# Another order of the expert slots in a unit, routing two units ahead, and the left sums of a block on its own partitions

## The chip, the cores and the metric

The kernel runs on one core of one Trainium2 chip. The metric is the device time of one execution in microseconds (us); the time before is the median of three runs.

## The reference

Two transformer blocks follow each other, for 256 tokens of width 2048 in float32. The change touches the expert layer of the second block (`peer_ffn`) and the place behind it, where the gate of the last layer is multiplied. Each token has 8 heads; for each head the reference picks 16 of 16,384 experts, takes the dot product of each expert's row `u` with the token, and adds up the rows `v` weighted by a gate.

```python
def peer_ffn(x, w_peer_q, peer_subkeys, peer_u, peer_v):
    q = (x @ w_peer_q).reshape(B, S, PEER_HEADS, 2, PEER_HALF)
    s = jnp.einsum('bshcd,hcnd->bshcn', q, peer_subkeys)
    top_s, top_i = lax.top_k(s, PEER_TOPK)
    cand = top_s[..., 0, :, None] + top_s[..., 1, None, :]
    ...
    best_s, best_c = lax.top_k(cand, PEER_TOPK)
    i1 = jnp.take_along_axis(top_i[..., 0, :], best_c // PEER_TOPK, axis=-1)
    i2 = jnp.take_along_axis(top_i[..., 1, :], best_c % PEER_TOPK, axis=-1)
    experts = i1 * N_KEYS + i2
    gates = jax.nn.softmax(best_s, axis=-1)
    ...
        u = peer_u[ec]
        act = jax.nn.gelu(jnp.einsum('tkd,td->tk', u, xc))
        return jnp.einsum('tk,tkd->td', gc * act, peer_v[ec])

    h = h + peer_ffn(rms_norm_2(h, ffn_norm[l]), ...)
    gate = jax.nn.sigmoid(rms_norm_2(h, ple_norm[l]) @ w_ple_gate[l])
    h = h + gate * (p[l] @ w_ple_proj[l])
```

The 16 experts of a head come out of `top_k` in the order of their gates: rank 0 has the largest, rank 15 the smallest. The inputs make the softmax steep, so that many gates of high rank are zero in float32.

## The kernel before

Most of the kernel is a row of matrix products whose weights stream from HBM (`gemm`, L343): each weight tile is loaded by SP, split into a rounded part by ACT (`h_...`, L361) and a rest by DVE (`l_...`, L362), and three matmuls of PE (L371 to L373) use them. `w_pg` is the last of these products and comes right behind the expert layer.

The expert layer is `peer` (L1310). It works in 4 blocks `u` of 64 tokens and in 4 pairs of heads `g`, which gives 16 units, `(0, 0)`, `(0, 1)` and so on; this document numbers them 0 to 15. In a unit, partitions 0 to 63 hold the 64 tokens for the first head of the pair and partitions 64 to 127 the same tokens for the second. A unit has 16 slots. Slot `j` handles one expert for each of the 128 partitions: rank `j` on the lower half and rank `(j + 8) % 16` on the upper half, since `route` writes the upper half's lists with the two groups of eight exchanged (L1478 to L1480). The slots are taken in the order 0, 8, 1, 9, 2, 10 up to 7, 15.

`slot` (L1386) does the work of one slot:

- POOL gathers 128 rows of 16 KB (`u` and `v` of an expert side by side) into one of `UVB` = 6 buffers `uvb` (L1390). A row whose gate is below the smallest normal float gets an index out of bounds, and the gather skips it. The first three slots of either group of eight in unit 0 skip nothing, so that all six buffers hold finite numbers.
- DVE multiplies the 2048 columns of `u` by the token `xg` and sums them (L1394). This document calls it the product of a slot.
- ACT takes the gelu, multiplies by the gate, and writes the result on a diagonal `dgs` (L1395 to L1398).
- PE multiplies `dgs` with the 2048 columns of `v` and adds to `acc_e` in PSUM (L1403). The left 1024 columns go to partitions 0 to 63 of `acc_e`, the right ones to 64 to 127.

POOL's queue holds nothing but the gathers in this stage, and they are issued in the order of the slots; a gather waits until PE is done with the slot six before it, whose buffer it fills.

`route` (L1418) finds the experts of a unit: four matmuls, then about 35 small DVE instructions for the two `top_k` and the look-up of indices, and a softmax. It is a generator, and `peer` runs a step of it after slots 0, 1, 3, 4, 6 and 7 for the unit to come. The order of the program text does not set the order of instructions, though: a scheduler places them, engine by engine, by its own estimate of when each is ready.

`block_x` (L1357) writes the tokens of a block, scaled, into `xg` and copies them to the other half of the partitions by a move on SP's queue. `block_out` (L1370) ends a block. A block `u` belongs to token half `t = u // 2` and stands on partitions `a * 64` to `a * 64 + 63` of `h`, with `a = u % 2`. ACT copies the half of `acc_e` that lies on the other partitions to `mv` (L1376), SP moves it over (L1377), and DVE adds both halves to `h`, 1024 columns each (L1379, L1380). For an odd block the half that has to be moved is the left one. `half_out` (L1382) squares and sums 512 columns of a token half (ACT, L340), transposes them on PE (L1412) and splits them by ACT and DVE (L309, L310) into the operands of `w_pg`; token half 0 is done inside the last unit's loop, half 1 behind it.

Of the kernel before, what the change touches and what calls it, by code (L numbers as in the profile page):

```python
# [13 lines left out]
ALU = mybir.AluOpType  # L14
# [251 lines left out]
class Net:  # L266
# [1043 lines left out]
    def peer(self):  # L1310

        nc, F, tc = self.nc, self.F, self.tc
        with tc.tile_pool(name="stg", bufs=2) as self.stg, tc.tile_pool(name="gat", bufs=1) as gat:
            self.gat = gat
            self.lists = {}
            for _ in self.route(0, 0):  # L1320
                pass
            xg = {0: self.block_x(0)}
            uv = [gat.tile([P, 2 * D], F32, tag=f"uv{i}", name=f"uvb{i}") for i in range(UVB)]
            junk = F(mybir.dt.bfloat16, (P, D))
            ssqp = self.small([P, 2, 4], keep="ssqe")
            order = [r + 8 * i for r in range(8) for i in range(2)]
            units = [(u, g) for u in range(4) for g in range(4)]
            acc = {}
            slot = 0
            for i, (u, g) in enumerate(units):  # L1330
                if g == 0:
                    acc[u] = self.psa.tile([P, 1024], F32, tag="acc", name=f"acc_e{u}")
                if g == 3 and u < 3:
                    xg[u + 1] = self.block_x(u + 1)
                later = self.route(*units[i + 1]) if i < 15 else iter(())
                for k, j in enumerate(order):
                    self.slot(u, g, j, uv[slot % UVB], xg[u], junk, acc[u], k == 0, k == 15)
                    slot += 1
                    if k in (0, 1, 3, 4, 6, 7):
                        next(later, None)  # L1340
                    if g == 0 and k == 2 and u:
                        self.block_out(u - 1, acc[u - 1])
                    if i == 15 and k in (3, 6, 9, 12):
                        if k == 3:
                            F.free(*self.qT, *self.sk, *self.gf)
                            n = Ops(F, 16, self.fp)
                        self.half_out(n, ssqp, 0, k // 3 - 1)
                for _ in later:
                    pass
            self.block_out(3, acc[3])  # L1350
            for c in range(4):
                self.half_out(n, ssqp, 1, c)
            F.free(junk)
        self.dump("x5", self.h)
        self.n4, self.rs4 = n, self.res_rs(ssqp)

    def block_x(self, u):  # L1357

        nc = self.nc
        t, a = u // 2, u % 2  # L1360
        x = self.gat.tile([P, D], F32, tag="xg", bufs=2, name=f"xg{u}")
        s, o = slice(a * 64, a * 64 + 64), slice(64 - a * 64, 128 - a * 64)
        for i in range(2):
            c = slice(i * 1024, (i + 1) * 1024)
            nc.vector.scalar_tensor_tensor(x[s, c], self.h[s, t, c], self.rs3[s, t:t + 1], self.gf[i][s], op0=ALU.mult,
                                           op1=ALU.mult)
        nc.sync.dma_start(x[o], x[s])
        return x

    def block_out(self, u, acc):  # L1370

        nc = self.nc
        t, a = u // 2, u % 2
        s, o = slice(a * 64, a * 64 + 64), slice(64 - a * 64, 128 - a * 64)
        e = self.gat.tile([P, 1024], F32, tag="mv", name=f"mv{u}")
        nc.scalar.copy(e[o], acc[o])  # L1376
        nc.sync.dma_start(e[s], e[o])  # L1377
        own, far = self.h[s, t, a * 1024:(a + 1) * 1024], self.h[s, t, (1 - a) * 1024:(2 - a) * 1024]
        nc.vector.tensor_tensor(own, acc[s], own, op=ALU.add)  # L1379
        nc.vector.tensor_tensor(far, e[s], far, op=ALU.add)  # L1380

    def half_out(self, n, ssqp, t, c):  # L1382
        self.sq_acc(self.h[:, t, c * 512:(c + 1) * 512], ssqp[:, t, c:c + 1])
# [2 lines left out]
    def slot(self, u, g, j, b, xg, junk, acc, begin, end):  # L1386
        nc, stg = self.nc, self.stg
        nm = f"{u}_{g}_{j}"
        idx, gate = self.lists[u, g]
        nc.gpsimd.indirect_dma_start(out=b, out_offset=None, in_=self.ap["uv"],  # L1390
                                     in_offset=bass.IndirectOffsetOnAxis(ap=idx[:, j:j + 1], axis=0),
                                     bounds_check=N_EXPERTS - 1, oob_is_err=False)
        a = stg.tile([P, 4], F32, tag="act", bufs=8, name=f"act{nm}")
        nc.vector.scalar_tensor_tensor(junk, b[:, :D], 1.0, xg, op0=ALU.mult, op1=ALU.mult, accum_out=a[:, 0:1])  # L1394
        nc.scalar.activation(a[:, 2:3], a[:, 0:1], AF.Gelu_apprx_tanh)  # L1395
        nc.scalar.activation(a[:, 3:4], a[:, 2:3], AF.Copy, scale=gate[:, j:j + 1])
        dg = stg.tile([P, 64], F32, tag="dgs", bufs=6, name=f"dgs{nm}")
        nc.scalar.activation(dg, self.c("id2"), AF.Copy, scale=a[:, 3:4])  # L1398
        first, last = g == 0 and begin, g == 3 and end
        for c in range(2):  # L1400
            for i in range(2):
                o = D + i * 1024 + c * 512
                nc.tensor.matmul(acc[i * 64:(i + 1) * 64, c * 512:(c + 1) * 512], dg, b[:, o:o + 512],  # L1403
                                 start=first, stop=last)

    def half_ops(self, ops, t, g, gname):
# [154 lines left out]
```

## Time and profile before

| | |
|---|---|
| three runs | 3237.61, 3239.88, 3243.05 us; median 3239.88 |
| the profiled execution, its own time | 3243.22 us |
| span of the profile (first to last instruction) | 3241.5 us |
| busy PE, DVE, ACT, POOL | 2879.1, 2164.7, 1438.7, 544.7 us |
| granted TensorE clock, mean | 0.966 |
| expert stage, first to last product L1394 | 2260.5 to 3123.3 us of the span |
| units 0, 1 to 8, 9 to 15 | 81.8, 428.9, 352.1 us |

The profile is of one execution. A share of busy time is a mean over the stage or window that it is given for. A row of a timeline has its start in us from the start of the span, its length, engine, line, operation, and in brackets the idle time of that engine before it and what ended it. `PEclk` is the granted clock of TensorE as a share of the full one.

### The profile page before, as it was taken

The page shows a single profiled execution, that of the slowest core. Times are in us where ns is not written, and L with a number is a line of the kernel's source. Part 1 is how long each engine was busy: PE and PEld are TensorE (multiplying, and loading weights), DVE is VectorE, ACT ScalarE, POOL GpSimd, SP SyncE. Part 2 cuts the span into 40 slices and gives each one's busy share as a digit, 9 for nine tenths or more (in the row PEclk, how much of TensorE's full clock was granted, in tenths as well). Part 3 has the DMA queues.
Part 4 walks back from the last instruction along what each step waited for, and adds up shares of the span by engine and source line. Part 5 has one row for each costly group of instructions (what it writes and reads, how often), then busy time and mean ns, then how long its engine had stood idle before and what let it go on. Part 6 is the DMA issues. An engine that isn't in the chain of part 4 may idle for free. (4 is left out here: it accounts for less than half of the span.)

```text
span 3241.5 us, 45843 instructions
## 1 busy us (share of the span) xinstructions
PE 2879.1 (89%) x17372; PEld 2268.3 (70%) x17372; DVE 2164.7 (67%) x3089; ACT 1438.7 (44%) x2464; POOL 544.7 (17%) x320
## 2 busy tenths in 40 slices
PE   8999999999999999999999999996566666666668
PEld 8888888989898998999999998896111111111136
DVE  7769666554545455686444577656989788877765
ACT  5446665434444444575434444542333233322244
POOL 0000000000000000011000021000355445564611
PEclk9999999999999999999999999998798988999999
DMA  7645564666666666656666545764688888878874
GB/s 261 182 150 188 157 183 143 184 193 183 193 185 192 183 189 185 185 173 185 184 182 182 158 148 164 213 184 150 259 313 309 304 331 284 332 294 332 319 257 142
DMA packets 156397, 691.86 MB, mean 213 GB/s; under 512 B 34127, under 2 KB 36431, under 8 KB 139855
## 3 DMA queue, kind: packets, MB, share of 16 engines
q1 hardware_dynamic: 119312, 425.64, 43.2%
q0 software_dynamic: 36864, 263.29, 21.7%
q8 instruction: 137, 2.24, 0.3%
q14 instruction: 84, 0.69, 0.1%
HBM read 955.12 MB, written 4.19 MB: 296 GB/s over the span
## 5 line engine op out<-in xcount | busy, mean ns | idle before, releaser
L1403 PE MATMUL acc_e<-uvb,dgs 128*64 128x512 f32 x2048 | 554.0, 672 | 303.5 <-ACT dgs L1398 303.5
L1394 DVE SCALAR_TENSOR_TENSOR f<-uvb,xg 128x2048 bf16<-128x2048 f32 x256 | 586.5, 2291 | 136.6 <-DMA uvb<-in_uv,idx 122.4
L1403 PEld LDWEIGHTS acc_e<-uvb,dgs 128*64 128x64 f32 x2048 | 138.2, 149 | 710.1 <-ACT dgs L1398 523.7
L1390 POOL DMA_INDIRECT uvb<-in_uv,idx x256 | 431.6, 1686 | 669.3 <-PE acc_e L1403 319.5
L1395 ACT ACTIVATE act<-act 128x1 f32<-128x1 f32 x256 | 51.9, 203 | 544.2 <-DVE f L1394 544.1
L381 PE MATMUL acc_w_up<-f,l_w_up 128*128 128x256 f32 x1024 | 289.9, 283 | 0.0
L378 PE MATMUL acc_w_up<-f,h_w_up 128*128 128x256 f32 x1024 | 289.9, 283 | 0.0
L380 PE MATMUL acc_w_up<-f,h_w_up 128*128 128x256 f32 x1024 | 289.8, 283 | 0.0
L362 DVE TENSOR_TENSOR l_w_up<-r_w_up,h_w_up 128x1024 fp32r<-128x1024 f32 x128 | 165.8, 1295 | 175.7 <-PE acc_w_up L381 153.1
L362 DVE TENSOR_TENSOR l_w_down<-r_w_down,h_w_down 128x1024 fp32r<-128x1024 f32 x128 | 161.2, 1260 | 162.2 <-PE acc_w_down L372 133.4
L361 ACT CAST h_w_down<-r_w_down 128x1024 fp32r<-128x1024 f32 x128 | 135.1, 1055 | 197.8 <-PE acc_w_down L373 168.5
L361 ACT CAST h_w_up<-r_w_up 128x1024 fp32r<-128x1024 f32 x128 | 134.7, 1052 | 196.6 <-PE acc_w_up L380 175.6
L371 PE MATMUL acc_w_down<-h_w_down,f 128*128 128x512 f32 x512 | 199.6, 390 | 0.0
L372 PE MATMUL acc_w_down<-l_w_down,f 128*128 128x512 f32 x512 | 199.5, 390 | 0.0
L373 PE MATMUL acc_w_down<-h_w_down,f 128*128 128x512 f32 x512 | 199.2, 389 | 0.0
L380 PEld LDWEIGHTS acc_w_up<-f,h_w_up 128*128 128x128 f32 x1024 | 196.6, 192 | 0.1
L378 PEld LDWEIGHTS acc_w_up<-f,h_w_up 128*128 128x128 f32 x1024 | 196.6, 192 | 0.1
L381 PEld LDWEIGHTS acc_w_up<-f,l_w_up 128*128 128x128 f32 x1024 | 196.6, 192 | 0.0
L584 POOL TENSOR_TENSOR f<-f 128x1024 f32<-128x1024 f32 x16 | 30.3, 1894 | 802.9 <-ACT f L583 802.9
L373 PEld LDWEIGHTS acc_w_down<-h_w_down,f 128*128 128x128 f32 x512 | 96.1, 188 | 19.9
L372 PEld LDWEIGHTS acc_w_down<-l_w_down,f 128*128 128x128 f32 x512 | 96.1, 188 | 19.8
L371 PEld LDWEIGHTS acc_w_down<-h_w_down,f 128*128 128x128 f32 x512 | 96.1, 188 | 19.7
(555 smaller groups left out, 7812.2 us busy)
## 6 DMA issues: line engine op xcount, KB each, us to landing
r_w_up<-in_w_up SPq DMA_DIRECT2D x128, 512.0 KB, 3.7
r_w_down<-in_w_down SPq DMA_DIRECT2D x128, 512.0 KB, 4.1
r_w_qkv<-in_w_qkv SPq DMA_DIRECT2D x48, 512.0 KB, 3.7
r_w_xbc<-in_w_xbc SPq DMA_DIRECT2D x32, 512.0 KB, 4.1
r_w_xr<-in_w_xr SPq DMA_DIRECT2D x32, 512.0 KB, 3.7
r_w_yr<-in_w_yr SPq DMA_DIRECT2D x32, 512.0 KB, 3.6
r_w_gr<-in_w_gr SPq DMA_DIRECT2D x32, 512.0 KB, 3.6
r_w_ro<-in_w_ro SPq DMA_DIRECT2D x32, 512.0 KB, 3.6
```

Of the source, the lines that this page charges most:

```text
L361: nc.scalar.copy(wh, raw)
L362: nc.vector.tensor_sub(wl, raw, wh.bitcast(F32))
L371: nc.tensor.matmul(o, xh[:, s], h, start=first, stop=False)
L372: nc.tensor.matmul(o, xh[:, s], l, start=False, stop=False)
L373: nc.tensor.matmul(o, xl[:, s], h, start=False, stop=fin)
L378: nc.tensor.matmul(o, wh[:, s], xh, start=first and b % 2 == 0, stop=False, skip_group_check=True)
L380: nc.tensor.matmul(o, wh[:, s], xl, start=False, stop=False, skip_group_check=True)
L381: nc.tensor.matmul(o, wl[:, s], xh, start=False, stop=fin, skip_group_check=True)
L1390: nc.gpsimd.indirect_dma_start(out=b, out_offset=None, in_=self.ap["uv"], in_offset=bass.IndirectOffsetOnAxis(ap=idx[:, j:j + 1], axis=0), ...
L1394: nc.vector.scalar_tensor_tensor(junk, b[:, :D], 1.0, xg, op0=ALU.mult, op1=ALU.mult, accum_out=a[:, 0:1])
L1395: nc.scalar.activation(a[:, 2:3], a[:, 0:1], AF.Gelu_apprx_tanh)
L1403: nc.tensor.matmul(acc[i * 64:(i + 1) * 64, c * 512:(c + 1) * 512], dg, b[:, o:o + 512], start=first, stop=last)
```

## The change

The slots of units 1 to 15 are taken in the order 0, 15, 8, 7, 1, 14, 9, 6, 2, 13, 10, 5, 3, 12, 11, 4; unit 0 keeps its order. Routing is written two units ahead: unit 0 runs the steps for units 1 and 2, one after each slot, and unit `i` those for unit `i + 2`, after slots 1, 3, 5, 8, 10 and 13. `half_out` of token half 0 moves from the last unit to the one before. In an odd block the two halves of `acc_e` change places, so that the left sums always lie on the block's own partitions and the right ones are moved; and the sums to `h` are made in four pieces of 512 columns, left ones first.

```diff
@@ -1323,7 +1324,7 @@
             uv = [gat.tile([P, 2 * D], F32, tag=f"uv{i}", name=f"uvb{i}") for i in range(UVB)]
             junk = F(mybir.dt.bfloat16, (P, D))
             ssqp = self.small([P, 2, 4], keep="ssqe")
-            order = [r + 8 * i for r in range(8) for i in range(2)]
+            even = [0, 15, 8, 7, 1, 14, 9, 6, 2, 13, 10, 5, 3, 12, 11, 4]
             units = [(u, g) for u in range(4) for g in range(4)]
             acc = {}
             slot = 0
@@ -1332,15 +1333,15 @@
                     acc[u] = self.psa.tile([P, 1024], F32, tag="acc", name=f"acc_e{u}")
                 if g == 3 and u < 3:
                     xg[u + 1] = self.block_x(u + 1)
-                later = self.route(*units[i + 1]) if i < 15 else iter(())
-                for k, j in enumerate(order):
+                later = self.routes(units[i + 2:i + 3] if i else units[1:3])
+                for k, j in enumerate(even if i else [r + 8 * h for r in range(8) for h in range(2)]):
                     self.slot(u, g, j, uv[slot % UVB], xg[u], junk, acc[u], k == 0, k == 15)
                     slot += 1
-                    if k in (0, 1, 3, 4, 6, 7):
+                    if i == 0 or k in (1, 3, 5, 8, 10, 13):
                         next(later, None)
                     if g == 0 and k == 2 and u:
                         self.block_out(u - 1, acc[u - 1])
-                    if i == 15 and k in (3, 6, 9, 12):
+                    if i == 14 and k in (3, 6, 9, 12):
                         if k == 3:
                             F.free(*self.qT, *self.sk, *self.gf)
                             n = Ops(F, 16, self.fp)
@@ -1354,6 +1355,11 @@
         self.dump("x5", self.h)
         self.n4, self.rs4 = n, self.res_rs(ssqp)
 
+    def routes(self, units):
+        for u in units:
+            yield from self.route(*u)
+            yield
+
     def block_x(self, u):
 
         nc = self.nc
@@ -1375,9 +1381,9 @@
         e = self.gat.tile([P, 1024], F32, tag="mv", name=f"mv{u}")
         nc.scalar.copy(e[o], acc[o])
         nc.sync.dma_start(e[s], e[o])
-        own, far = self.h[s, t, a * 1024:(a + 1) * 1024], self.h[s, t, (1 - a) * 1024:(2 - a) * 1024]
-        nc.vector.tensor_tensor(own, acc[s], own, op=ALU.add)
-        nc.vector.tensor_tensor(far, e[s], far, op=ALU.add)
+        for c in range(4):
+            hc = self.h[s, t, c * 512:(c + 1) * 512]
+            nc.vector.tensor_tensor(hc, (acc if c < 2 else e)[s, (c % 2) * 512:(c % 2 + 1) * 512], hc, op=ALU.add)
 
     def half_out(self, n, ssqp, t, c):
         self.sq_acc(self.h[:, t, c * 512:(c + 1) * 512], ssqp[:, t, c:c + 1])
@@ -1400,7 +1406,8 @@
         for c in range(2):
             for i in range(2):
                 o = D + i * 1024 + c * 512
-                nc.tensor.matmul(acc[i * 64:(i + 1) * 64, c * 512:(c + 1) * 512], dg, b[:, o:o + 512],
+                p = 64 * (i ^ (u % 2))
+                nc.tensor.matmul(acc[p:p + 64, c * 512:(c + 1) * 512], dg, b[:, o:o + 512],
                                  start=first, stop=last)
 
     def half_ops(self, ops, t, g, gname):
```

The lines behind L1316 are shifted by one to seven in the new kernel; the product is L1400 there.

On DVE, the rows at the start of unit 3 (the names `act_3_8` and so on give head pair and slot of a product; `tv`, `tiu`, `cand`, `best`, `bc` are routing), before:

```order
L1496 MAX tv_24230<-mr_24251 128x8
L1497 MAX_INDEX tiu_24231<-tv_24230,mr_24251 128x8
L1441 CAST tif_24283<-tiu_24231 128x32
L1443 TENSOR_TENSOR cand_24285<-tv_24230 128x256
L1493 MAX best_24287<-cand_24285 128x8
L1394 SCALAR_TENSOR_TENSOR f_301_21721,act_3_8_22581<-uvb_21716,xg_21711 128x2048
L1493 MAX tv_24782<-sc_24780 128x8 x2
L1494 MAX_INDEX bc_24288<-best_24287,cand_24285 128x8
L1494 MAX_INDEX tiu_24783<-tv_24782,sc_24780 128x8 x2
L1394 SCALAR_TENSOR_TENSOR f_301_21721,act_3_1_22600<-uvb_21717,xg_21711 128x2048
L1394 SCALAR_TENSOR_TENSOR f_301_21721,act_3_9_22613<-uvb_21718,xg_21711 128x2048
L1394 SCALAR_TENSOR_TENSOR f_301_21721,act_3_2_22638<-uvb_21719,xg_21711 128x2048
```

and now:

```order
L1503 MAX tv_24032<-mr_24073 128x8
L1504 MAX_INDEX tiu_24033<-tv_24032,mr_24073 128x8
L1448 CAST tif_24105<-tiu_24033 128x32
L1450 TENSOR_TENSOR cand_24107<-tv_24032 128x256
L1500 MAX best_24109<-cand_24107 128x8
L1400 SCALAR_TENSOR_TENSOR f_301_21721,act_3_15_22632<-uvb_21716,xg_21711 128x2048
L1500 MAX tv_24587<-sc_24585 128x8 x2
L1501 MAX_INDEX bc_24110<-best_24109,cand_24107 128x8
L1501 MAX_INDEX tiu_24588<-tv_24587,sc_24585 128x8 x2
L1400 SCALAR_TENSOR_TENSOR f_301_21721,act_3_8_22660<-uvb_21717,xg_21711 128x2048
L1400 SCALAR_TENSOR_TENSOR f_301_21721,act_3_7_22673<-uvb_21718,xg_21711 128x2048
L1400 SCALAR_TENSOR_TENSOR f_301_21721,act_3_1_22692<-uvb_21719,xg_21711 128x2048
```

The products have another slot in each place; the routing instructions between them are of the same kind and stand in the same places.

On ACT, behind the last slot of the expert stage (`mv` is the copy of `block_out`, `junk` the squares, `f_...<-ho_ple_norm` an operand half of `w_pg`, `h_w_pg_0` the rounded first weight tile), before:

```order
L1376 COPY mv_26140<-acc_e_25036 64x1024
L340 ACTIVATE junk_26145,ssqe_21722<-h 128x512
L340 ACTIVATE junk_26160,ssqe_21722<-h 128x512
L309 ACTIVATE f_302_25923<-ho_ple_norm_1_0_26147,pv 128x128
L340 ACTIVATE junk_26175,ssqe_21722<-h 128x512
L309 ACTIVATE f_304_25979<-ho_ple_norm_1_1_26162,pv 128x128
L309 ACTIVATE f_302_25923<-ho_ple_norm_1_0_26147,pv 128x128
L340 ACTIVATE junk_26190,ssqe_21722<-h 128x512
L361 CAST h_w_pg_0_26249<-r_w_pg_0_26248 128x1024
```

and now, from the eighth row behind that copy on:

```order
L309 ACTIVATE f_302_25721<-ho_ple_norm_1_0_26155,pv 128x128
L309 ACTIVATE f_306_25833<-ho_ple_norm_1_2_26185,pv 128x128
L309 ACTIVATE f_304_25777<-ho_ple_norm_1_1_26170,pv 128x128
L317 ACT_TABLE_LOAD
L317 ACTIVATE s_26218<-s_26217 128x2
L309 ACTIVATE f_308_25889<-ho_ple_norm_1_3_26200,pv 128x128
L309 ACTIVATE f_302_25721<-ho_ple_norm_1_0_26155,pv 128x128
L309 ACTIVATE f_306_25833<-ho_ple_norm_1_2_26185,pv 128x128
L309 ACTIVATE f_304_25777<-ho_ple_norm_1_1_26170,pv 128x128
L309 ACTIVATE f_308_25889<-ho_ple_norm_1_3_26200,pv 128x128
L361 CAST h_w_pg_0_26257<-r_w_pg_0_26256 128x1024
L309 ACTIVATE f_306_25833<-ho_ple_norm_1_2_26185,pv 128x128
```

The cast of the first weight tile stood eighth behind the copy; now it stands eighteenth, behind eight more operand halves, a table load and a root.

## Rows read from the trace of the kernel before

**Rows 1.** The page, DMA queues: packets, MB, share of 16 engines.

```profile
q0 software_dynamic: 36864, 263.29, 21.7%
```

**Rows 2.** Windows of units 1 to 8: header, and the sum of the eight.

```profile
core 0: us, PE busy (x) PEld busy (x) DVE busy (x) ACT busy (x) POOL busy (x), PEclk, DMA share, GB/s
...
sum 428.90, PE 280.79 PEld 71.27 DVE 373.81 ACT 145.18 POOL 218.14; mean PE 35.10 PEld 8.91 DVE 46.73 ACT 18.15 POOL 27.27
```

**Rows 3.** Windows of units 9 to 15: the sum of the seven.

```profile
sum 352.10, PE 231.33 PEld 58.77 DVE 263.38 ACT 98.82 POOL 180.55; mean PE 33.05 PEld 8.40 DVE 37.63 ACT 14.12 POOL 25.79
```

**Rows 4.** Windows, units 9 to 15: sums of four quarters; unit 11's third.

```profile
sum 91.90, PE 57.93 PEld 15.21 DVE 66.22 ACT 25.59 POOL 45.55; mean PE 8.28 PEld 2.17 DVE 9.46 ACT 3.66 POOL 6.51
...
sum 95.10, PE 57.61 PEld 14.17 DVE 65.44 ACT 22.14 POOL 44.33; mean PE 8.23 PEld 2.02 DVE 9.35 ACT 3.16 POOL 6.33
...
2898.30:2910.60 12.30, 8.27 (x30) 2.04 (x26) 9.21 (x9) 3.29 (x12) 6.88 (x4) 0.86 0.57 196
...
sum 82.10, PE 54.31 PEld 13.49 DVE 64.46 ACT 22.59 POOL 39.47; mean PE 7.76 PEld 1.93 DVE 9.21 ACT 3.23 POOL 5.64
...
sum 83.10, PE 61.48 PEld 15.91 DVE 67.26 ACT 28.59 POOL 51.19; mean PE 8.78 PEld 2.27 DVE 9.61 ACT 4.08 POOL 7.31
```

**Rows 5.** The same for units 1-3 and 5-7; unit 7's third quarter.

```profile
sum 82.30, PE 47.33 PEld 12.96 DVE 80.71 ACT 17.16 POOL 16.37; mean PE 7.89 PEld 2.16 DVE 13.45 ACT 2.86 POOL 2.73
...
sum 68.30, PE 52.73 PEld 12.85 DVE 55.16 ACT 24.46 POOL 57.08; mean PE 8.79 PEld 2.14 DVE 9.19 ACT 4.08 POOL 9.51
...
2689.60:2699.60 10.00, 8.62 (x32) 2.39 (x32) 9.20 (x8) 3.40 (x13) 5.42 (x4) 0.83 0.69 247
sum 69.00, PE 47.09 PEld 11.73 DVE 55.31 ACT 18.34 POOL 40.48; mean PE 7.85 PEld 1.95 DVE 9.22 ACT 3.06 POOL 6.75
...
sum 85.60, PE 58.01 PEld 14.35 DVE 79.24 ACT 40.11 POOL 53.47; mean PE 9.67 PEld 2.39 DVE 13.21 ACT 6.68 POOL 8.91
```

**Rows 6.** Timeline of DVE at the start of unit 1: its first three products.

```profile
2342.26 2.28 DVE L1394 SCALAR_TENSOR_TENSOR f<-uvb,xg 128x2048 bf16<-128x2048 f32 x1
...
2347.96 2.27 DVE L1394 SCALAR_TENSOR_TENSOR f<-uvb,xg 128x2048 bf16<-128x2048 f32 x1
...
2351.47 2.27 DVE L1394 SCALAR_TENSOR_TENSOR f<-uvb,xg 128x2048 bf16<-128x2048 f32 x1
```

**Rows 7.** Timeline around 2970: two products, the first one's matmuls, the next issue.

```profile
2967.86 2.29 DVE L1394 SCALAR_TENSOR_TENSOR f<-uvb,xg 128x2048 bf16<-128x2048 f32 x1
...
2970.25 2.29 DVE L1394 SCALAR_TENSOR_TENSOR f<-uvb,xg 128x2048 bf16<-128x2048 f32 x1
...
2971.16 1.94 PE L1403 MATMUL acc_e<-uvb,dgs 128*64 128x512 f32 x8 [0.45 <-ACT dgs L1398]
...
2973.71 2.09 POOL L1390 DMA_INDIRECT uvb<-in_uv,idx  x1 [0.30 <-issue]
```

**Rows 8.** First gather (POOL, timeline), its product, and DMA view of 2254 to 2276.

```profile
2252.10 1.16 POOL L1390 DMA_INDIRECT uvb<-in_uv,idx  x1 [242.69 <-DVE tv L1493]
...
2260.54 2.29 DVE L1394 SCALAR_TENSOR_TENSOR f<-uvb,xg 128x2048 bf16<-128x2048 f32 x1 [0.87 <-DMA uvb<-in_uv,idx]
...
DMA packets 624, 9.17 MB, mean 417 GB/s; under 512 B 64, under 2 KB 64, under 8 KB 64
```

**Rows 9.** Chain of waits (first three) and ACT's timeline behind the last slot.

```profile
3126.25 1.01 ACT mv L1376
3127.28 2.83 DMA mv<-mv
3130.14 1.23 DVE h L1380
...
3134.97 1.04 ACT L361 CAST h_w_pg<-r_w_pg 128x1024 fp32r<-128x1024 f32 x1
...
3135.92 1.13 ACT L309 ACTIVATE f<-ho_ple_norm,pv 128x128 fp32r<-128x128 f32 x4
...
3137.07 1.28 ACT L317 ACT_TABLE_LOAD   x1
```

## The prediction, made before the run

> **What bounds the kernel now.** The page comes first: the software queue, which carries the gathers, moved 263.29 MB [rows 1]. Every edit lies in the expert stage or just behind it, so I cut that stage into its sixteen units, each from the first product L1394 of one unit to that of the next, and read the windows view of them. The reader is to see that DVE has two kinds of unit. Units 1 to 8 last 428.9 us with DVE busy 373.81, units 9 to 15 last 352.1 with DVE busy 263.38 [rows 2, 3]: 55.1 and 88.7 us of waiting. A unit of the first kind holds some 45 us of DVE work, one of the second some 37; the difference is routing.
>
> Next I cut each unit into four quarters of four slots. In units 9 to 15 DVE idles 25.7, 29.7, 17.6 and 15.8 us in the four quarters, summed over seven units (window minus DVE busy) [rows 4]. So it waits most where the gathers are largest, but the lightest quarter still idles 2.5 us a unit, and there the DMA share is down to 0.57 in unit 11 [rows 4]. Not all of the waiting is load, then. In units 1 to 3 and 5 to 7 the same sums are 1.6, 13.1, 13.7 and 6.4 [rows 5]: the first quarter hardly waits, since routing fills DVE there while gathers land.
>
> The timeline shows it: at the start of unit 1 the products begin 5.7 and 3.5 us apart instead of the bare 2.4, because routing stands between, and none of them waited for a DMA [rows 6]. What landed during this burst feeds the products behind it.
>
> Last, the ring of six buffers. A product is followed by three ACT instructions and eight matmuls: one began at 2967.86, the next 2.39 later, its matmuls ended at 2973.10, 5.2 after its start, and then POOL issued for 2.09 [rows 7]. At one product per 2.39 us the ring allows 6 x 2.39 = 14.3 us a turn; 5.2 + 0.3 + 2.1 are spent, which leaves 6.7 for landing. A full gather of 2.10 MB needed 7.3 (issue ended at 2253.26, product began at 2260.54), and the transfers run at 417 GB/s while six such gathers are queued [rows 8].
>
> **Sizes of the slots.** Rows with a vanished gate are skipped. Evaluating the reference's routing on its inputs gives the share of rows kept by rank: 1.00, 0.95, 0.88, 0.78 for ranks 0 to 3, 0.37 for rank 8, 0.13 for rank 15. Slot j has rank j below and (j+8) mod 16 above, so slots 0 and 8 fetch about 87 rows, 1 and 9 82, 2 and 10 74, and 7 and 15 only 37. In the old order the first six slots of a unit ask for 486 rows and the last six for 254; in the new order any six ask for about 370. The total is unchanged (16,066 rows of 16 KB are the 263.29 MB).
>
> **Routing two units ahead: 0 us.** The order of the built programs settles this. The routing burst stands at the same places on DVE in both, behind the last product of a unit and its first two; the scheduler had already run it far ahead. What the new code interleaves over slots 1 to 13 does not appear there. Nothing is added to or taken from POOL or SP: 256 gathers, four moves of xg and four of mv, at the same slots. Half of the operands of tokens 0 to 127 now come a few slots earlier in unit 8, with the same instructions, hidden in its 53.53 us of DVE work; if that cover went it would only change places.
>
> **The order of the slots, units 9 to 15: -7 us.** No burst hides anything here. If every quarter idled like the two lighter ones, (25.7 + 29.7) - (17.6 + 15.8) = 22 us would go; that is the lower bound, and 0 the upper. An evened quarter carries more than the light ones do, and these idle 2.4 us a unit anyway, so I take a third: -7.
>
> **The order of the slots, units 1 to 8: +11 us.** The burst lets six slots land. They used to be the heaviest; now 116 rows fewer (1.9 MB) are fetched under it, and have to be fetched later beside products. At 417 GB/s that is 4.6 us a unit at most. At the low end the second and third quarters would idle like a light quarter of units 9 to 15, 2.4 each, against (13.1 + 13.7) / 6 = 4.5 together now: +0.3. With the mean quarter of units 9 to 15 (88.7 / 28 = 3.2) it is +1.9. Since the DMA has slack in these quarters (a share of 0.69 in unit 7's third) [rows 5], I take 1.4, between the two: 8 x 1.4 = 11, bounds +2 and +36. Unit 0 keeps its order.
>
> **The left sums stay: +1 us.** Four sums of 512 columns in place of two of 1024 cost nothing new: one of 1024 takes 1.23 [rows 9], so one of 512 about 0.6 (an estimate from that row). At the end of block 3 the left sums no longer wait for the move: copy 1.01 and move 2.83 [rows 9], -3.8 if all of it were saved. But PE transposes all four chunks ahead of the first w_pg matmul, two of them still behind the move, which ends when it did. And ACT now has the cast h_w_pg_0 behind seventeen instructions instead of seven after the copy: a table load of 1.28, a root and eight more operand halves (four take 1.13) come before it [rows 9]. By hand from the end of the sums (3126.25): the last square at +6.2, three halves +7.1, table load and root +8.6, five halves +10.2, cast +11.2; before, it ended at 3136.0, +9.8 [rows 9]. So +1.4, bounds -3.8 and +2.4; the early transposes may give a little back, and I take +1. The chain of waits runs on PE from the first w_pg matmul to the last, so a late start is not hidden.
>
> **Sum.** -7 + 11 + 1 = +5. The profiled execution took 3243.22, so the sum gives 3248.2 for it; the median of the three runs is 3239.88, 3.3 lower, and +5 on it is 3245. About 0.2% (6.5 us) is what a measurement of this kernel can tell from no change; 3245 is inside it.
>
> By the Trainium skill, "DMA: Bandwidth & Descriptors", section "Anatomy of one DMA", a software DMA costs about 2.0 us plus its bytes over 436 GB/s. That would give a mean slot (1.03 MB) 2.4 us of streaming, an estimate from that page, so evened gathers would just keep up with DVE. By that rate the trace agrees, with 417 GB/s [rows 8]. The same page, in "Why a DMA increments its semaphore by 16 and not by 1", says that a gather has landed only when each of its 16 engines has finished; that speaks against evening by totals, and the 2.5 us of idle at light load fit it [rows 4].
>
> **Rivals.**
> - **A, the load was the waiting.** Units 9 to 15 gain the whole 22 us, and units 1 to 8 lose only 0.3 each: -22 + 2 + 1 = -19, 3221. For it: the heavy halves of the units hold 55.4 of the 88.8 us of idle [rows 4]. Against: the light halves hold the rest.
> - **A2, DVE alone sets the pace.** All 143.8 us of waiting goes but 0.1 a slot (240 slots): -120, 3120. This is where the streaming rule cited above would lead. Against: light quarters wait too.
> - **B, the ring's turn binds.** Heavy slots 9, 2 and 10 now come after the burst's six. If such a slot lands later than the 6.7 us that the ring allows, DVE waits: not at all if the streaming part scales with its rows (2.3 + 5.0 x 85/128 = 5.6), 7.3 - 6.7 = 0.6 if it lands as late as a full gather [rows 8]. At three slots of eight units that is +14 beside the low end of +2; units 9 to 15 meet the same wait and gain nothing; with +1 at the end +17, 3257. It decides from a landing of 6.7 us on. For it: light quarters wait though the DMA is free [rows 4], so landing is more than load. Against: the light slots between leave room.
> - **C, the change does nothing.** Partly so: the routing's place is unchanged, which is in the sum.
>
> **Chances and range.** My forecast (+5, own range 3238 to 3252) 0.45, of which 0.38 falls within 0.2%; A 0.20; A2 0.04; B 0.31, of which 0.03 falls within. So faster 0.24, same 0.41, slower 0.35. The range reaches to A and a little beyond B: 3220 to 3260; A2 and B's bound of +36 stay outside.
>
> **What would show it.** Right: units 9 to 15 shorter by a few us each, most in their first halves; units 1 to 3 and 5 to 7 longer by 1 to 2, their second and third quarters idling more; routing between the same products; the first w_pg matmul no earlier behind the last sum. A shows as units 9 to 15 near 47 us with units 1 to 8 unchanged, B as units 1 to 8 longer by 3 or more. A routing burst spread over slots 1 to 13, or gathers at over 400 GB/s in all quarters, would make the reasoning itself wrong.

## The result and the profile after

The changed kernel takes 3262.21 us (median of four runs, 3260.3 to 3265.52); the kernel before, run beside it, takes 3239.45 (3237.61 to 3243.05). The ratio of the first to the second is 1.007 with a 95% interval of 1.0053 to 1.0087: about 0.7% **slower**. The forecast was 3245 with a range up to 3260; the result lies 2 us above that range.

The profiled execution took 3260.3 us, 17.1 more than that of before. The windows view of units 1 to 8, then of units 9 to 15, of the changed kernel (columns as in [rows 2]):

```profile
2624.10:2678.30 54.20, 39.14 (x128) 10.33 (x128) 45.25 (x79) 17.16 (x55) 21.72 (x16) 0.75 0.80 304
...
sum 450.80, PE 304.77 PEld 79.80 DVE 373.66 ACT 146.23 POOL 212.06; mean PE 38.10 PEld 9.97 DVE 46.71 ACT 18.28 POOL 26.51
...
sum 347.50, PE 238.02 PEld 59.97 DVE 263.58 ACT 98.84 POOL 181.90; mean PE 34.00 PEld 8.57 DVE 37.65 ACT 14.12 POOL 25.99
```

The work of DVE is what it was: 373.66 us beside 373.81 [rows 2], 263.58 beside 263.38 [rows 3]. Only its waiting changed. Units 1 to 8 take 21.9 us more, units 9 to 15 4.6 less, and the rest about nothing: the sum is the 17 us. The first row is unit 6; the third number from its end is the granted clock, 0.75, where unit 6 of before had 0.90:

```profile
2612.70:2664.10 51.40, 34.31 (x128) 8.32 (x128) 45.30 (x78) 17.15 (x55) 30.31 (x16) 0.90 0.86 316
```

The quarters, units 9 to 15, first to fourth (answer to [rows 4]):

```profile
sum 75.20, PE 55.22 PEld 14.37 DVE 66.27 ACT 22.23 POOL 33.98; mean PE 7.89 PEld 2.05 DVE 9.47 ACT 3.18 POOL 4.85
...
sum 89.40, PE 66.48 PEld 16.92 DVE 65.58 ACT 26.88 POOL 55.69; mean PE 9.50 PEld 2.42 DVE 9.37 ACT 3.84 POOL 7.96
...
sum 87.20, PE 55.71 PEld 13.53 DVE 64.39 ACT 22.33 POOL 50.52; mean PE 7.96 PEld 1.93 DVE 9.20 ACT 3.19 POOL 7.22
...
sum 95.70, PE 60.61 PEld 15.15 DVE 67.33 ACT 27.39 POOL 41.71; mean PE 8.66 PEld 2.16 DVE 9.62 ACT 3.91 POOL 5.96
```

DVE idles 8.9, 23.8, 22.8 and 28.4 us (window less DVE busy). The first quarter gave up 17 us of waiting and the last took on 13: the waits moved rather than went. In units 1 to 3 and 5 to 7 (answer to [rows 5]):

```profile
sum 82.10, PE 48.46 PEld 13.41 DVE 80.56 ACT 17.10 POOL 15.73; mean PE 8.08 PEld 2.23 DVE 13.43 ACT 2.85 POOL 2.62
...
sum 73.10, PE 62.97 PEld 15.74 DVE 55.23 ACT 25.33 POOL 55.28; mean PE 10.50 PEld 2.62 DVE 9.20 ACT 4.22 POOL 9.21
...
2594.90:2608.50 13.60, 8.71 (x34) 2.39 (x32) 9.25 (x9) 3.38 (x12) 6.15 (x4) 0.87 0.97 376
sum 76.60, PE 47.73 PEld 12.85 DVE 55.35 ACT 18.60 POOL 30.90; mean PE 7.95 PEld 2.14 DVE 9.22 ACT 3.10 POOL 5.15
...
sum 93.80, PE 64.42 PEld 16.01 DVE 79.19 ACT 38.99 POOL 46.88; mean PE 10.74 PEld 2.67 DVE 13.20 ACT 6.50 POOL 7.81
```

The idle times are 1.5, 17.9, 21.3 and 14.6 us, 20.5 us more than before in six units. The prediction relied on slack of the DMA in these quarters and read it from one, unit 7's third with a share of 0.69 [rows 5]. That was the emptiest of the six third quarters; the others stood at 0.76 to 0.90 (the last number but one of a row; unit 6 of before):

```profile
2637.70:2649.30 11.60, 7.74 (x32) 1.93 (x32) 9.23 (x9) 2.62 (x10) 9.47 (x5) 1.00 0.90 314
```

Now the six stand at 0.85 to 0.97, unit 5's highest (its row above).

**What happens under the burst.** Two stretches of 14 us cover the burst of unit 6, from just before its first product to the seventh, in the kernel before and in the changed one:

```profile
2613.00:2627.00 14.00, 8.96 (x24) 2.02 (x24) 13.72 (x31) 3.27 (x12) 2.91 (x2) 0.63 0.80 324
```

```profile
2624.00:2638.00 14.00, 8.62 (x20) 2.06 (x22) 13.73 (x32) 2.97 (x11) 2.55 (x2) 0.54 0.63 238
```

DVE does the same in both; the DMA moves 324 GB/s in one and 238 in the other, 1.2 MB less. The DMA view of the second stretch shows where the rest went, in 40 slices of 0.35 us each:

```profile
DMA  9999996969979553531202011009931667474845
```

The engines are busy, then nearly stop in the middle, with nine slices in a row at 0.2 or less, while POOL (timeline of its gathers, changed kernel) issues almost nothing:

```profile
2622.70 0.99 POOL L1396 DMA_INDIRECT uvb<-in_uv,idx  x1 [2.37 <-DVE s L1474]
2631.34 1.57 POOL L1396 DMA_INDIRECT uvb<-in_uv,idx  x1 [7.65 <-PE acc_e L1410]
2637.02 1.74 POOL L1396 DMA_INDIRECT uvb<-in_uv,idx  x1 [4.11 <-PE acc_e L1410]
2639.80 1.29 POOL L1396 DMA_INDIRECT uvb<-in_uv,idx  x1 [1.04 <-PE acc_e L1410]
```

All six buffers are asked for by 2623.7. The next gathers wait 7.65 and 4.11 us for matmuls, which wait for products, which stand between routing instructions. The kernel before has the same two holes at this place (its POOL, then its DMA view of the first stretch):

```profile
2620.00 1.58 POOL L1390 DMA_INDIRECT uvb<-in_uv,idx  x1 [7.65 <-PE acc_e L1403]
2625.67 1.76 POOL L1390 DMA_INDIRECT uvb<-in_uv,idx  x1 [4.08 <-PE acc_e L1403]
```

```profile
DMA  9694979969497996949665352599949298455738
```

But its six slots hold 496 rows there against 378 now (the reference's routing on its inputs), so its DMA still has work when POOL resumes: it slows, and no slice falls below 0.2. Behind the burst DVE then waits for the slots it has no lead on (timeline of DVE, changed kernel, L1400):

```profile
2650.62 2.29 DVE L1400 SCALAR_TENSOR_TENSOR f<-uvb,xg 128x2048 bf16<-128x2048 f32 x1 [3.38 <-DMA uvb<-in_uv,idx]
...
2653.01 2.29 DVE L1400 SCALAR_TENSOR_TENSOR f<-uvb,xg 128x2048 bf16<-128x2048 f32 x1
...
2656.08 2.29 DVE L1400 SCALAR_TENSOR_TENSOR f<-uvb,xg 128x2048 bf16<-128x2048 f32 x1 [0.77 <-DMA uvb<-in_uv,idx]
...
2664.06 2.29 DVE L1400 SCALAR_TENSOR_TENSOR f<-uvb,xg 128x2048 bf16<-128x2048 f32 x1 [3.29 <-DMA uvb<-in_uv,idx]
```

The product at 2650.62 is the ninth of the unit, the heavy slot 2 of 80 rows. Its gather is the last of the POOL rows above, issued at 2641.09: 9.5 us to the product, where the ring allows 6.7 [rows 7]. The light slot behind it waits for nothing; the heavy ones 10 and 3 wait again. Over units 1 to 8, DVE's products waited for gathers for 42.6 us before and for 65.4 now (view of the product's line, time and number of waits):

```profile
  DMA uvb<-in_uv,idx: 42.6, 42
```

```profile
  DMA uvb<-in_uv,idx: 65.4, 37
```

Added up by slot from the brackets of the timeline, 20.0 of the 65.4 stand in front of slot 2, 7.4 in front of slot 10, 10.8 of slot 3 and 11.5 of slot 11.

**Routing and the tail.** Unit 1 of the changed kernel starts as in [rows 6], 5.7 and 3.5 us apart:

```profile
2341.39 2.28 DVE L1400 SCALAR_TENSOR_TENSOR f<-uvb,xg 128x2048 bf16<-128x2048 f32 x1
...
2347.08 2.27 DVE L1400 SCALAR_TENSOR_TENSOR f<-uvb,xg 128x2048 bf16<-128x2048 f32 x1
...
2350.60 2.27 DVE L1400 SCALAR_TENSOR_TENSOR f<-uvb,xg 128x2048 bf16<-128x2048 f32 x1
```

Behind the last sum of the expert stage (its matmuls end at 3142.6; timeline of ACT and PE, answer to [rows 9]):

```profile
3149.61 1.28 ACT L317 ACT_TABLE_LOAD   x1
...
3152.27 1.07 ACT L361 CAST h_w_pg<-r_w_pg 128x1024 fp32r<-128x1024 f32 x1
...
3153.39 0.80 PE L371 MATMUL acc_w_pg<-h_w_pg,f 128*128 128x512 f32 x1 [4.11 <-ACT h_w_pg L361]
```

The cast ends 10.7 us behind the sums where it ended 9.8 behind them before, since a table load, a root and more operand halves now come before it on ACT.

### The profile page after: what moved, and what is told of

It reads as the page before. It is cut to its first block, busy times and chain, and to the rows that moved or that the text cites. A ratio compares the mean times of both kernels' runs of the same rounds, so it can differ in the third digit from the quotient of the medians.

```text
span 3258.5 us, 45860 instructions
## 1 busy us (share of the span) xinstructions
PE 2906.5 (89%) x17372; PEld 2275.2 (70%) x17372; DVE 2163.5 (66%) x3097; ACT 1440.6 (44%) x2464; POOL 539.2 (17%) x320
## 3 DMA queue, kind: packets, MB, share of 16 engines
q0 software_dynamic: 36864, 263.29, 21.8%
## 5 line engine op out<-in xcount | busy, mean ns | idle before, releaser
L1410 PE MATMUL acc_e<-uvb,dgs 128*64 128x512 f32 x2048 | 581.6, 707 | 291.6 <-ACT dgs L1404 291.0
L1400 DVE SCALAR_TENSOR_TENSOR f<-uvb,xg 128x2048 bf16<-128x2048 f32 x256 | 586.4, 2290 | 153.4 <-DMA uvb<-in_uv,idx 140.3
L1410 PEld LDWEIGHTS acc_e<-uvb,dgs 128*64 128x64 f32 x2048 | 146.2, 156 | 715.7 <-ACT dgs L1404 508.2
```

The lines of the kernel that those rows point to most:

```text
L1410: nc.tensor.matmul(acc[p:p + 64, c * 512:(c + 1) * 512], dg, b[:, o:o + 512], start=first, stop=last)
```

## The experiments

Three theories stood at the start. **F**: less is fetched under the burst and has to be paid for later. **K**: the new waits lower TensorE's clock, and slower matmuls keep buffers longer. **L**: the other edits take part. **B** is the prediction's rival, heavy slots behind light ones land too late for the ring; **R** says the same of every gather, whatever its size.

**1. The order alone**, on the kernel before:

```diff
-                for k, j in enumerate(order):
+                for k, j in enumerate(even if i else old):
```

> The kernel before with nothing but the new slot order in units 1 to 15. Theory F (what the routing burst no longer hides: 1.9 MB less are fetched under it, and units 1 to 8 pay for them later) and theory K (the new waits lower the granted clock, matmuls take longer, buffers come free later, and so on) both say that the order carries the whole loss: about 3262 us, units 1 to 8 about 451 us, units 9 to 15 about 347. Theory L (the left sums, the four pieces or the routing written two units ahead take part): clearly less, 3250 or below.

Measured: ratio 1.0053 (1.0037 to 1.007), median 3259.38 us. Units 1 to 8 in the windows view:

```profile
sum 450.20, PE 295.31 PEld 76.64 DVE 373.47 ACT 145.26 POOL 228.15; mean PE 36.91 PEld 9.58 DVE 46.68 ACT 18.16 POOL 28.52
```

The order carries the loss: 0.53% where the whole change has 0.70%, and the two intervals overlap.

**2. Everything but the order**, on the changed kernel:

```diff
-                for k, j in enumerate(even if i else [r + 8 * h for r in range(8) for h in range(2)]):
+                for k, j in enumerate([r + 8 * h for r in range(8) for h in range(2)]):
```

> The changed kernel with the old slot order in every unit: routing written two units ahead, left sums on their own partitions in four pieces, token half 0 one unit earlier. F and K: 3239 to 3242 us, units 1 to 8 about 429. L: 3250 or above.

Measured: 0.9994 (0.9982 to 1.0006). Units 1 to 8, and 9 to 15:

```profile
sum 429.50, PE 283.42 PEld 71.67 DVE 373.62 ACT 146.26 POOL 226.41; mean PE 35.43 PEld 8.96 DVE 46.70 ACT 18.28 POOL 28.30
...
sum 346.10, PE 224.44 PEld 56.88 DVE 263.61 ACT 98.81 POOL 169.17; mean PE 32.06 PEld 8.13 DVE 37.66 ACT 14.12 POOL 24.17
```

L falls. And units 9 to 15 take 346.1 us in the *old* order: the 352.1 of [rows 3] was not typical.

**3. The new order in units 9 to 15 alone:**

```diff
-                for k, j in enumerate(order):
+                for k, j in enumerate(even if i > 8 else old):
```

> The kernel before with the new order in units 9 to 15 alone, where no routing burst stands. F and K: units 1 to 8 as before, 429 us; units 9 to 15 347 to 348; 3235 us, some 5 below before. If the gain in units 9 to 15 was only carried over from the longer units before them, no gain: 3239.

Measured: 1.0004 (0.9992 to 1.0016), no gain. Units 1 to 8, and 9 to 15:

```profile
sum 432.00, PE 286.29 PEld 72.44 DVE 373.86 ACT 145.29 POOL 224.02; mean PE 35.79 PEld 9.06 DVE 46.73 ACT 18.16 POOL 28.00
...
sum 347.80, PE 233.63 PEld 60.71 DVE 263.21 ACT 98.83 POOL 175.96; mean PE 33.38 PEld 8.67 DVE 37.60 ACT 14.12 POOL 25.14
```

The expectation of a gain, taken from the profile's 352.1 and 347.5, missed. Units 9 to 15 take 347.4 to 348.2 us in the new order (four kernels), 345 to 348 in the old one in four other kernels, and 352.1 once.

**4. TensorE kept busy**, in the changed kernel:

```diff
+                    self.warm = ({15: 8, 0: 8, 1: 5, 2: 2}.get(k, 1) if 0 < 4 * u + g + k // 15 < 9 else 1) if i or k == 15 else 0
...
+        for _ in range(self.warm):
+            nc.tensor.matmul(self.wm[:64, :256], dg, xg[:, :256], start=True, stop=True)
```

> The changed kernel with idle matmuls behind each slot's own (256 columns into an unused bank: 8 behind the last slot of a unit and its first, 5 and 2 behind the next two, 1 behind the others), so that TensorE has fewer gaps in the units. K: the granted clock in units 1 to 8 goes from about 0.82 to near 1.0 and the loss goes with it: units 1 to 8 about 432 us, 3243. F: the clock may rise, but units 1 to 8 stay at 447 to 451, 3258 to 3262. If the clock does not rise, the run tells nothing of K.

Measured: 1.0068 (1.0046 to 1.009), median 3266.81 us. The scheduler moved routing from unit 0 into unit 1 here (DVE is busy 83.78 us in that unit), so units 3 to 7 are compared: this kernel (unit 6, sum, then unit 8 beside them), then the changed one (sum, unit 8):

```profile
2628.90:2682.60 53.70, 44.94 (x200) 18.60 (x199) 45.26 (x79) 17.15 (x55) 23.52 (x16) 1.00 0.82 306
...
sum 276.90, PE 227.97 PEld 94.38 DVE 229.66 ACT 86.70 POOL 122.68; mean PE 45.59 PEld 18.88 DVE 45.93 ACT 17.34 POOL 24.54
...
2734.70:2797.30 62.60, 49.29 (x208) 20.82 (x207) 53.56 (x93) 24.59 (x79) 28.38 (x15) 0.92 0.77 268
```

```profile
sum 279.90, PE 189.83 PEld 48.05 DVE 229.81 ACT 85.15 POOL 128.62; mean PE 37.97 PEld 9.61 DVE 45.96 ACT 17.03 POOL 25.72
...
2731.80:2792.20 60.40, 42.41 (x142) 12.56 (x144) 53.40 (x105) 26.77 (x80) 32.16 (x16) 0.77 0.83 284
```

The clock of these five units is granted at 0.97 to 1.00 in place of 0.75 to 0.84, unit 6 at the full 2.4 GHz throughout, and the units take 276.9 us in place of 279.9. Unit 8 takes 2.2 us more at a higher clock, and unit 2 takes 53.1 us in both kernels, so units 2 to 8 take 392.6 in place of 393.4: of the 18.6 us that the changed kernel loses there (before: 374.8), 0.8 come back. The idle matmuls take time on PE too, so this is a net figure. K is not the main cause; what makes the clock fall in these units, no run shows by itself.

**5. The lightest slots under the burst**, units 1 to 8 in the old order turned round:

```diff
-                for k, j in enumerate(order):
+                for k, j in enumerate(old[::-1] if 0 < i < 9 else old):
```

> The kernel before with the old order turned round in units 1 to 8 (15, 7, 14, 6 and so on, the lightest slots under the routing burst), units 9 to 15 as before. Theory F (what is not fetched under the burst is paid for later): the first six slots ask for about 254 rows where the old order asks for 486 and the new one for 370, so the loss doubles: units 1 to 8 about 472 us, 3283. Theory B (single heavy slots that come behind light ones land too late for the ring of six): the heavy slots now stand in one descending run at the end, none of them behind a light one but the neighbours are nearly equal; the loss is about that of the new order or less, 3262 at most.

Measured: 1.0116 (1.0096 to 1.0136), median 3281.12 us, units 1 to 8:

```profile
sum 467.00, PE 294.46 PEld 72.65 DVE 373.43 ACT 145.16 POOL 213.22; mean PE 36.81 PEld 9.08 DVE 46.68 ACT 18.15 POOL 26.65
```

This is near F's forecast: the loss is about twice that of the new order, and no heavy slot stands alone behind a light one here. B as the only cause falls.

**6. Six heavy slots under the burst, turns behind it:**

```diff
+            mix = [0, 8, 1, 9, 2, 10, 15, 3, 7, 11, 14, 4, 6, 12, 13, 5]
-                for k, j in enumerate(order):
+                for k, j in enumerate(mix if 0 < i < 9 else old):
```

> The kernel before, units 1 to 8 in the order 0, 8, 1, 9, 2, 10, 15, 3, 7, 11, 14, 4, 6, 12, 13, 5: the same six heavy slots under the burst, then light and heavy ones by turns. F: as before, units 1 to 8 429 to 434 us, 3240 to 3246. B: the heavier slots behind light ones wait, most of the loss comes back: units 1 to 8 440 or more, 3252 or more.

Measured: 1.0015 (1.0005 to 1.0025), units 1 to 8:

```profile
sum 437.40, PE 285.73 PEld 72.58 DVE 373.49 ACT 145.16 POOL 214.66; mean PE 35.72 PEld 9.07 DVE 46.69 ACT 18.15 POOL 26.83
```

Between the two: 437.4 us, where the three kernels with the old order there took 428.9, 429.5 and 432.0 (mean 430.1). So the sequence behind the burst costs some 7 us (4.9 by the ratio, 1.6 to 8.1), though the same is fetched under it. The waits are not where B has them. Added up by slot over units 1 to 8, 28.9 us of waiting for gathers stand in front of the lighter slots 15, 7, 14, 6 and 13, and 16.9 in front of the heavier 3, 11, 4, 12 and 5. The last four slots of a unit ask for 202 rows here and for 161 in the old order, and the waits in front of them are 21.2 and 8.3 us. Rows that come later in the unit explain this run at least as well as turns do; it does not tell the two apart.

**7. The new order's six under the burst, no turns behind it:**

```diff
+            mix = [0, 15, 8, 7, 1, 14, 9, 2, 10, 3, 11, 4, 12, 5, 13, 6]
```

> The kernel before, units 1 to 8 in the order 0, 15, 8, 7, 1, 14, 9, 2, 10, 3, 11, 4, 12, 5, 13, 6: the new order's six slots under the routing burst (370 rows), then the rest from heavy to light as in the old order, without turns. F alone (only what is fetched under the burst counts): half of the loss that the turned-round order showed, units 1 to 8 448 us. If the turns of heavy and light behind the burst are a part of the new order's loss (the run with six heavy slots and turns says 5 to 8 us): 440 to 444.

Measured: 1.0026 (1.0014 to 1.0037), units 1 to 8:

```profile
sum 439.50, PE 286.98 PEld 73.40 DVE 373.44 ACT 145.17 POOL 217.42; mean PE 35.87 PEld 9.17 DVE 46.68 ACT 18.15 POOL 27.18
```

F alone said 448; it is 439.5, so the lighter burst costs 9.4 of the 20.4 us that the new order costs units 1 to 8 (450.5, the mean of its two kernels, less 430.1). The new order differs from this run only behind the burst, and there it costs the other 11.0; by the ratios, 0.26 and 0.27 of 0.53%, each uncertain by 0.1 to 0.2. Neither is the whole. The waits in front of the heavy slots 2, 10, 3 and 11 are 28.6 us here and 49.0 in run 1, those in front of 6, 13, 5, 12 and 4 are 26.5 and 15.7.

The burst has no fixed price per row: this run fetches 116 rows fewer under it for 9.4 us, run 5 232 fewer for 36.9, four times as much for twice the rows. Why, stays open.

**8 and 9. Fewer rows**, in the kernel before and in the changed one:

```diff
-TINY = float(np.finfo(np.float32).tiny)
+TINY = 1e-24
```

> The kernel before with the threshold for a vanished gate raised from the smallest normal float to 1e-24: gates below it are set to zero and their rows are not fetched, so these summands are left out. 8,906 of the reference's gates remain where 15,770 were, so some 146 MB are fetched where 263 were. Ranks 0 and 8 of a slot still ask for all 64 rows of one half. F (volume sets the waits): the idle time of DVE in units 9 to 15 falls from about 87 us to below 30, and units 1 to 8 lose most of theirs: 3120 to 3150 us. R (the delay of single full gathers sets them): idle time in units 9 to 15 stays above 60, 3190 or more.

> The changed kernel with the same raised threshold, the same summands left out. F: with half the volume the order no longer matters, within 5 us of the old order with that threshold. R: the heavy slots behind light ones wait as before, 10 us or more above it.

Measured: 3147.1 us (ratio 0.9707, 0.9689 to 0.9726) and 3160.64 (0.9748, 0.9727 to 0.9769), with 152.76 MB gathered. Units 9 to 15, old order, then new:

```profile
sum 297.10, PE 224.50 PEld 57.69 DVE 263.45 ACT 98.84 POOL 207.21; mean PE 32.07 PEld 8.24 DVE 37.64 ACT 14.12 POOL 29.60
```

```profile
sum 300.20, PE 222.54 PEld 57.21 DVE 263.50 ACT 98.83 POOL 198.61; mean PE 31.79 PEld 8.17 DVE 37.64 ACT 14.12 POOL 28.37
```

In the old order DVE idles 33.7 us in these units where it idled 88.7, and its products wait for gathers for 18.4 us where they waited for 79.0 (before, then run 8):

```profile
  DMA uvb<-in_uv,idx: 79.0, 63
```

```profile
  DMA uvb<-in_uv,idx: 18.4, 17
```

So volume makes most of the waiting here, and R falls; F's "below 30" is missed by a little. But the order still costs 13.5 us (3160.64 less 3147.1), 9.1 of it in units 1 to 8 (396.5 against 387.4), where F alone had said 5 at most. There the products wait for gathers for 1.3 us in run 8 and for 8.9 in run 9:

```profile
  DMA uvb<-in_uv,idx: 1.3, 2
```

```profile
  DMA uvb<-in_uv,idx: 8.9, 9
```

All of the 8.9 stands in front of the heavy slots 2, 10, 3 and 11, and nothing in front of the light ones between them. The DMA was not full: of the quarters of units 1 to 3 and 5 to 7 in run 9 the fullest has a share of 0.74:

```profile
2619.70:2635.30 15.60, 10.15 (x44) 2.43 (x40) 13.30 (x32) 7.45 (x21) 8.29 (x7) 1.00 0.74 253
```

This is B's mechanism, heavy slots behind light ones that land too late, with a DMA that is not full. What part of the 11.0 us of run 7 it makes at the full volume, no run separates.

**10 to 12. Seven buffers**, in the kernel before, in the changed one, and in the changed one with the old order (the room comes from using the block's finished `xg` in place of `mv`):

```diff
-UVB = 6
+UVB = 7
...
-        e = self.gat.tile([P, 1024], F32, tag="mv", name=f"mv{u}")
+        e = self.xgs[u][:, :1024]
```

> The kernel before with seven gather buffers in place of six; the room comes from moving the copy mv into the token tile xg of the same block, which is done by then; one more pair of slots in unit 0 skips no rows. F (the gathers' volume sets the waits): in units 9 to 15 the idle time of DVE stays near 87 us, a few us less; units 1 to 8 lose part of their waits because one more slot lands under the burst, up to 20 us; 3215 to 3235. R (the turn of the ring, that is the delay of each gather, sets the waits): a turn gets 2.4 us longer, half or more of all waiting goes, also in units 9 to 15: below 3190.

> The changed kernel with seven gather buffers, the same way. F: the loss against seven buffers in the old order stays 15 to 25 us. R: it goes down to a few us, since the slack of the longer turn takes up the heavy slots.

> The changed kernel with the old slot order and seven gather buffers: the best of both so far. If the rest of the change is worth nothing either way, the same as seven buffers in the kernel before, 3198 to 3203 us.

Measured: 3200.82 us (0.9865, 0.9846 to 0.9884), 3217.42 (0.9922, 0.9903 to 0.9942) and 3206.54 (0.9898, 0.9876 to 0.992). Seven buffers in the kernel before, units 1 to 8 and 9 to 15:

```profile
sum 407.10, PE 280.11 PEld 72.03 DVE 373.50 ACT 145.40 POOL 229.10; mean PE 35.01 PEld 9.00 DVE 46.69 ACT 18.18 POOL 28.64
...
sum 331.00, PE 222.74 PEld 56.06 DVE 263.56 ACT 98.80 POOL 164.36; mean PE 31.82 PEld 8.01 DVE 37.65 ACT 14.11 POOL 23.48
```

This is the fastest version that leaves no summands out, 1.35% below the kernel before. It gains more than F had said and less than R had: waiting in units 9 to 15 goes from some 83 us (346.1 less 263.6 in run 2) to 67.4, and in units 1 to 8 from 55 to 33.6. The new order still costs 16.6 us with it, as F had said. Its waits in front of slot 2 in units 1 to 8 are gone (20.0 us with six buffers), but those in front of 10, 3 and 11 are not (29.0 of 32.5): a seventh buffer takes up one heavy slot and no more. The third kernel's interval overlaps the first's; 3206 was above what was expected, and whether the rest of the change costs a few us there stays open.

By the Trainium skill, "Perfetto Trace Analysis", section "Optimization Strategy", a gap that repeats on the engine that should be saturated can mean too little room for the next tile. Run 10 agrees: one buffer more took 1.35% off.

## Why the prediction was wrong, step by step

- **Routing two units ahead: 0.** Right. The products at the start of unit 1 stand apart as before, and run 2 lies between 0.18% below and 0.06% above the kernel before.
- **Units 9 to 15: -7.** Wrong, it is 0 (run 3: -2.6 to +5.2 us on the whole kernel). Two things failed. The step "these idle 2.4 us a unit anyway, so I take a third" had the waits of the heavy quarters as something that evening takes away; with the same volume to fetch, they moved into the last quarters. (The quarter that the text calls the lightest, with 2.5 us of idle a unit, is the third; the fourth idles 2.3, at DMA shares of 0.80 to 0.87 in units 9 to 14.) And the one profile that it was read from had these units 4 to 7 us longer than four other kernels with the same order, which is why the profile of after seemed to confirm the -7.
- **Units 1 to 8: +11.** The sign and the place were right, the size was half: +21.9 in the profile, 2.7 a unit where the step "I take 1.4, between the two" stood. Two things failed in it. Its reason, "the DMA has slack in these quarters", was read from the emptiest of six quarters (0.69, the others 0.76 to 0.90). And the sum has no term for what the new sequence does behind the burst, which costs 11.0 us (run 7 beside run 1). Part of that is rival B's mechanism, heavy slots behind light ones, as run 9 shows. The text weighed B *against* the forecast, as a case of its own; the two go on together. The lighter burst alone costs 9.4 us (run 7), near the +11, but with the slack misread and no fixed price per row (run 5) that is partly luck.
- **The tail: +1.** Right: the first `w_pg` matmul starts 0.9 us later behind the sums. The cast of its first weight tile ends 10.7 us behind the sums; by hand it was 11.2.
- **The rivals.** A (3221) and A2 (3120) fell: the waits moved. B (3257) came nearest in time, but its price was wrong in its parts: slots 9, 2 and 10 were priced at 0.6 us each, and over units 1 to 8 they wait 0, 20.0 and 7.4 us (0.7, 3.4 and 2.8 before), while slots 3 and 11, with 22.3, were not priced. Its sign, units longer by 3 us or more, was met in the six units of [rows 5] (20.5 / 6 = 3.4) and not over all eight (2.7); its claim that units 9 to 15 gain nothing held. C held for the routing. The estimate from the Trainium skill, "DMA: Bandwidth & Descriptors", section "Anatomy of one DMA", by which evened gathers would just keep up with DVE, is not borne out: units 9 to 15 idle 83.9 us with them.
- **The range.** It stopped a little above B, since it was made of cases that exclude each other. Forecast and B together would have been 11 + 14 + 0 + 1 = 26, or 3266; this sum is made after the fact, and B's 14 in it is the price just called wrong.

The sign "gathers at over 400 GB/s in all quarters" did not show: of the quarters of units 1 to 3 and 5 to 7 in the changed kernel the fullest has 376. What stays open is how a gather's delay comes about when the DMA has slack, as in run 9; no run took a single gather apart.

## What to carry to other kernels

Where an engine is busy with other work for a while and a ring of buffers fills up, what can be prefetched in that time is counted in slots, not in bytes: put the largest transfers there, and look first whether another buffer fits. Causes of waiting that don't exclude each other are terms to add, not rivals to choose between. And a term read from one profile is no better than that profile's spread: units 9 to 15 took 344.9 to 352.1 us here in five kernels with the same order in them.

## What the runs showed that was not expected

The granted clock of TensorE was not the cause of anything large here. Keeping it at 0.97 to 1.00 in place of 0.75 to 0.84 over five units changed their 279.9 us by 3, and with the units on either side of them the gain was 0.8.

With the volume down from 263.29 to 152.76 MB, and the DMA at shares of 0.52 to 0.67, DVE still waited 18.4 us for gathers in units 9 to 15. A part of the gathers' delay stays when there is less to fetch; whether more bandwidth would take it away, no run shows.
